# Seven block products for a quarter of the K tiles of a feed forward's gate and up

## The chip, the core and the metric

The program runs on one core of a Trainium2 chip. It is one kernel, launched once. Time is device microseconds of that core; a kernel is timed in several runs and the median is given. Here the kernel before takes 2408.33 us (three runs, 2407.59 to 2408.73).

Engines: TensorE (PE) multiplies matrices, VectorE (DVE) and ScalarE (ACT) work on elements, GpSimd (POOL) helps them, and SyncE (SP) issues DMA transfers. Each engine takes its instructions in the order in which they were written for it and waits on semaphores for the others.

## The reference

256 tokens of width 2048 pass through two layers of a first block (a hybrid of banded attention, gated linear attention and memory attention, with a layer norm) and one layer of a second block. The change is in the last step of the second block, and two more places in it come up later: the first projection of the second block and the step from `w_o` to the feed forward.

```python
D_MODEL, SEQ = 2048, 256
D_FF = -(-(8 * D_MODEL) // (3 * 256)) * 256          # 5632
# second block, after its two mixers gave y_a and y_b
h = rms_norm(x, norm_mix_pre);  proj = h @ w_in
...
merged = jax.nn.sigmoid(g_a) * y_a + jax.nn.sigmoid(g_b) * y_b
x = x + rms_norm(merged @ w_o, norm_mix_post)
h = rms_norm(x, norm_ffn_pre)
gate, up = jnp.split(h @ w_ffn_in, 2, axis=-1)
x = x + rms_norm((jax.nn.silu(gate) * up) @ w_ffn_down, norm_ffn_post)
```

Everything is fp32.

## The kernel before

**Numbers.** An fp32 product is made of three matmuls on rounded operands. A matrix tile is split into a high half (a rounding cast on ACT, L272 for weights) and a low half (the rest, a subtraction on DVE, L273); then x_high·w_high, x_high·w_low and x_low·w_high are added up in PSUM (L330 to L332). Activations are split the same way (L354, L355) behind transposes on PE (L377), four of 128x128 into one PSUM bank.

**Tiling.** A product is a list of jobs, one for each 512 columns of a weight matrix, with the 2048 rows as 16 K tiles of 128. The weights stream from HBM: a part is two K tiles by 512 columns, 512 KB, in one slot of 128x1024. For each K tile there are three matmuls for tokens 0 to 127 (t = 0) and three for tokens 128 to 255 (t = 1), so a part is 12 matmuls of 512 columns. The gate and up of the feed forward are eleven units of 512 columns, each a gate job and an up job of 8 parts; the first unit is called the head. Down products follow each group of units.

**Order.** `Builder.run` writes out all instructions in one go. It walks over units (a part, and which t). Before a unit's matmuls it makes sure that the part is loaded and split; after that `ahead` loads and splits parts in advance, as long as the rules allow: at most N_RAW = 4 loaded and not yet split, at most N_HL = 6 held as split halves, and enough free slots of the 41. Side work (transposes, norms, silu) runs in generators that `pump` steps after each unit, when their time on a planner's clock has come. So the place of an instruction in its engine's order is fixed by when `run`, `ahead` and `pump` reach it.

**Apart.** Where a product begins right behind another whose normalised output it reads, the first tokens are ready sooner than the others. There a run of parts is done apart: first all parts for t = 0 alone, 6 matmuls each, then the same parts for t = 1 (key "in" from `w_out` of the second layer to `w_in` of the second block, "ffn" from `w_o` to the feed forward's head, and the last down columns). The split halves have to be kept for the second pass. In these units `ahead` has its own rule:

```python
if len(units[u][2]) == 1:
    cap, reserve, far = len(parts), 0, u + NEAR
```

The cap on held halves is lifted, no slots are kept in reserve, and splits reach at most NEAR = 8 units ahead. The finishing work between the two products runs on DVE, ACT and POOL: L1467 (squares with a row sum), L1477, L446, L447 (the reciprocal root), L1481 (scaling), L1501 (gain) and, behind that, four transposes; then L542, four squares of the residual for each half of the tokens. In "in" it is a layer norm: L1108, L1109, the transposes, and later L1113 (DVE), L1117 (ACT), L1121 (POOL).

Of the kernel before, what the change touches and what calls it, by code (L numbers as in the profile page):

```python
# [45 lines left out]
FS = 8000  # L46
FH = 4000
# [10 lines left out]
class Job:  # L58
# [11 lines left out]
    def __init__(self, kind, w, c0, cn, act, post, pre=None, order=None, k0=0, apart=None):  # L70
# [3 lines left out]
        self.apart = apart or (None, 0, 0)  # L74
# [23 lines left out]
class Builder:  # L98
    def __init__(self, ctx, tc, a):
        self.tc, self.nc, self.a = tc, tc.nc, a  # L100
        pool = lambda name, bufs, **kw: ctx.enter_context(tc.tile_pool(name=name, bufs=bufs, **kw))
        self.const = pool("const", 1)
        self.tmp = pool("tmp", 2)
        self.small = pool("small", 4)
        self.psm = pool("psm", 2, space=bass.MemoryType.PSUM)
        self.pss = pool("pss", 4, space=bass.MemoryType.PSUM)
        self.dram = pool("dram", 1, space=bass.MemoryType.DRAM)
        self.free = list(range(N_SLOT))
        self.act = self.const.tile([P, NKT, 2, S], F32R, tag="act", name="act")
# [3 lines left out]
        self.clock = 0.0  # L113
        self.n = 0
# [6 lines left out]
    def alloc(self, n=1, dt=F32):  # L121
        tries = 0
        while len(self.free) < n:
            tries += 1
            assert self.side and tries < 1000, "out of slots"
# [87 lines left out]
    def run(self, jobs, loaded_first, split_first):  # L213
# [4 lines left out]
        for job in jobs:  # L218
            n = NKT if job.kind == "n" else min(1024 // job.cn, 4)
            name, lo, hi = job.apart  # L220
            for j, k in enumerate(range(0, len(job.order), n)):
                key = name if lo <= j < hi else None
                if not (key and groups and groups[-1][0] == key):
                    groups.append((key, []))
                groups[-1][1].append(len(parts))
                parts.append((job, job.order[k:k + n], k))
        for key, mine in groups:
            for ts in ((0,), (1,)) if key else ((0, 1),):
                for i in mine:
                    job, kts, k = parts[i]  # L230
                    units.append((job, i, ts, k == 0 and ts[0] == 0, k + len(kts) == len(job.order), mine[-1]))
# [6 lines left out]

        def pieces(i, n):

            return [slice(k, k + 1) for k in range(n)] if i == 0 else [slice(0, n)]

        def do_load(i):
            job, kts, _ = parts[i]
# [8 lines left out]

        def do_split(i):
            job, kts, _ = parts[i]
            n = len(kts) * job.cn
# [19 lines left out]
        def room(u):  # L276
# [4 lines left out]
            if loaded <= end:  # L281
                return len(self.free) > 2
            coming = 2 * max(0, end + 1 - split) - sum(r <= end for r in raws)
            return len(self.free) - coming > HOLD

        def ahead(u):
# [17 lines left out]
        for u, (job, i, ts, first, last, _) in enumerate(units):  # L304
            while split <= i:
                if loaded == split:
# [4 lines left out]
            if len(ts) == 2:  # L311
                ahead(u)
            if first:
                if job.pre:
                    job.pre()
            if first:
                job.ps = self.psm.tile([P, 2, 512], F32, tag="main", name=f"main_j{jobs.index(job)}")
# [3 lines left out]
            for k, kt in enumerate(kts):  # L321
# [4 lines left out]
                if job.kind == "x":  # L326
                    for t in ts:
                        o = job.ps[:, t, :job.cn]
                        rows = slice(t * P, t * P + P)
                        nc.tensor.matmul(o, xh[:, rows], h[:, k, :], start=st, stop=False)  # L330
                        nc.tensor.matmul(o, xh[:, rows], l[:, k, :], start=False, stop=False)  # L331
                        nc.tensor.matmul(o, xl[:, rows], h[:, k, :], start=False, stop=en)  # L332
# [15 lines left out]
            self.pump()  # L348

# [31 lines left out]
def network(ctx, tc, a):  # L381
# [76 lines left out]
    def feeder(act, t, delay, gap=1500):  # L458
        yield delay
        while act.left[t]:  # L460
            act.feed_next(t)
            yield gap

# [1028 lines left out]
    def mix_done(ids, t):  # L1492
# [13 lines left out]
        else:  # L1506
            start_late(fact, [f[0], f[1]], x1res, None, lambda: B.release(ids + f["wi"]), False)
# [36 lines left out]
    def hidden(c, gi):  # L1544

        yield FH
# [32 lines left out]
    for g, n in enumerate((4, 4, 3)):  # L1579
        for c in range(n):  # L1580
            c0 = 512 * (at + c)
            head = (g, c) == (0, 0)
            jobs.append(Job("x", wf, c0, 512, fact, first_gate if head else post_gate2, apart=("ffn", 0, 8) if head else None))
# [63 lines left out]
```

## Time and profile before

| | |
|---|---|
| median of three runs | 2408.33 us (2407.59 to 2408.73) |
| the profiled run, its own time | 2407.96 us |
| span in the profile | 2406.2 us |
| PE busy | 2390.2 us, 99 %, 12105 matmuls and transposes |
| DVE busy | 1476.3 us, 61 % |
| ACT busy | 1099.0 us, 46 % |
| POOL busy | 400.8 us, 17 % |
| from HBM | 454.18 MB read, 192 GB/s over the span |
| DMA engines, share of time on SP's queue | 60.7 % |

All times are of one profiled execution. An engine is busy while it executes an instruction; issuing DMAs and waiting on semaphores isn't counted. Matmuls overlap in the array and their ends are modelled, so the distance between two starts tells what one costs. An idle time is put down to the instruction whose semaphore came last. The granted clock is TensorE's, as a share of full speed.

### The profile page before, as it was taken

What the parts mean: (1) busy time and instruction counts of PE and PEld (TensorE: products, weight loads), DVE (VectorE), ACT (ScalarE), POOL (GpSimd) and SP (SyncE); (2) the same over time, 40 slices, a digit from 0 to 9 for tenths busy, and PEclk for the clock granted to TensorE, in tenths of its full rate; (3) what the DMA queues carried; (4) which work ended last, traced back from release to release, by engine and by line L of the source; (5) the groups of instructions that cost most, each with busy time, mean ns of one, the idle gap of its engine ahead of it and who ended that gap; (6) DMA issues with size and microseconds to landing.
All of it is one profiled execution on the core that took longest, in us unless ns stands there. A gap on an engine that the chain in (4) does not pass through costs nothing. (4 is left out here: it accounts for less than half of the span.)

```text
span 2406.2 us, 31460 instructions
## 1 busy us (share of the span) xinstructions
PE 2390.2 (99%) x12105; PEld 2015.7 (84%) x12105; DVE 1476.3 (61%) x1671; ACT 1099.0 (46%) x1472; POOL 400.8 (17%) x601
## 2 busy tenths in 40 slices
PE   9999999999999999999999999999999999999998
PEld 8888888888888888888888888888888888888886
DVE  6587567666855667766765656657545544554455
ACT  6444445345454553655544544445434423443433
POOL 0330010004400110364764340001000000000000
PEclk9999999999999999999999999999999999999999
DMA  9646567674656674854654666675755655555653
GB/s 327 184 149 184 173 187 262 209 239 133 188 160 186 206 252 156 275 164 125 185 161 146 201 185 194 202 242 186 242 176 180 194 185 193 201 183 177 209 192 131
DMA packets 313911, 464.64 MB, mean 193 GB/s; under 512 B 21961, under 2 KB 161569, under 8 KB 313761
## 3 DMA queue, kind: packets, MB, share of 16 engines
q1 hardware_dynamic: 312528, 459.48, 60.7%
q8 instruction: 95, 1.56, 0.3%
q0 software_dynamic: 640, 2.10, 0.2%
q10 hardware_dynamic: 592, 1.06, 0.1%
q14 instruction: 56, 0.45, 0.1%
HBM read 454.18 MB, written 8.40 MB: 192 GB/s over the span
## 5 line engine op out<-in xcount | busy, mean ns | idle before, releaser
L273 DVE TENSOR_TENSOR slot<-slot,slot 128x1024 fp32r<-128x1024 f32 x810 | 1006.9, 1287 | 190.5 <-ACT slot L272 186.7
L272 ACT CAST slot<-slot 128x1024 fp32r<-128x1024 f32 x810 | 807.8, 1046 | 266.2 <-DVE slot L273 123.6
L339 PE MATMUL main_j<-act,slot 128*128 128x512 f32 x1824 | 651.0, 400 | 0.0
L330 PE MATMUL main_j<-slot,act 128*128 128x512 f32 x1608 | 636.2, 396 | 0.0
L331 PE MATMUL main_j<-slot,act 128*128 128x512 f32 x1608 | 626.4, 390 | 2.8 <-DVE slot L273 2.8
L332 PE MATMUL main_j<-slot,act 128*128 128x512 f32 x1608 | 626.8, 390 | 0.0
L340 PE MATMUL main_j<-act,slot 128*128 128x256 f32 x1824 | 509.9, 280 | 0.0
L339 PEld LDWEIGHTS main_j<-act,slot 128*128 128x128 f32 x1824 | 342.4, 188 | 80.2 <-issue 1.1
L331 PEld LDWEIGHTS main_j<-slot,act 128*128 128x128 f32 x1608 | 302.4, 188 | 63.6 <-DVE slot L273 3.8
L332 PEld LDWEIGHTS main_j<-slot,act 128*128 128x128 f32 x1608 | 301.8, 188 | 63.9
L330 PEld LDWEIGHTS main_j<-slot,act 128*128 128x128 f32 x1608 | 302.2, 188 | 61.3 <-ACT slot L272 0.5
L340 PEld LDWEIGHTS main_j<-act,slot 128*128 128x128 f32 x1824 | 344.1, 189 | 0.8
L330 PE MATMUL main_j<-slot,slot 128*128 128x512 f32 x600 | 236.1, 394 | 0.0
L332 PE MATMUL main_j<-slot,slot 128*128 128x512 f32 x600 | 233.8, 390 | 0.0
L331 PE MATMUL main_j<-slot,slot 128*128 128x512 f32 x600 | 233.6, 389 | 0.0
L447 POOL TENSOR_TENSOR rsl<-rsl,nhalf 128x1 f32<-128x1 f32 x8 | 6.2, 775 | 991.7 <-DVE rsl L446 991.7
L332 PEld LDWEIGHTS main_j<-slot,slot 128*128 128x128 f32 x600 | 112.6, 188 | 23.8
L330 PEld LDWEIGHTS main_j<-slot,slot 128*128 128x128 f32 x600 | 112.7, 188 | 23.0
L331 PEld LDWEIGHTS main_j<-slot,slot 128*128 128x128 f32 x600 | 112.8, 188 | 22.5
L674 POOL TENSOR_TENSOR slot<-slot 128x128 f32<-128x128 f32 x144 | 79.2, 581 | 191.9 <-PE main_j L339 92.8
L354 ACT CAST slot<-bank 128x512 fp32r<-128x512 f32 (+1 forms) x30 | 15.9, 529 | 177.7 <-PE bank L377 170.7
L813 POOL TENSOR_TENSOR slot<-slot,tz 128x512 f32<-128x512 f32 x20 | 25.8, 1290 | 397.8 <-DVE tz L812 397.8
(193 smaller groups left out, 1738.4 us busy)
## 6 DMA issues: line engine op xcount, KB each, us to landing
slot<-in_w_in_dram SPq DMA_DIRECT2D x384, 512.0 KB, 4.0
slot<-in_w_ffn_in_dram SPq DMA_DIRECT2D x176, 512.0 KB, 4.6
slot<-in_w_ffn_down_dram SPq DMA_DIRECT2D x88, 512.0 KB, 4.6
slot<-in_w_out_dram SPq DMA_DIRECT2D x64, 512.0 KB, 4.7
slot<-in_w_o_dram SPq DMA_DIRECT2D x32, 512.0 KB, 4.5
slot<-in_w_mem_kv_dram SPq DMA_DIRECT2D x31, 512.0 KB, 5.9
slot<-in_w_up_b_dram SPq DMA_DIRECT2D x16, 512.0 KB, 4.6
slot<-in_w_up_a_dram SPq DMA_DIRECT2D x16, 512.0 KB, 4.4
```

The source lines that it names most:

```text
L272: nc.scalar.copy(h, src)
L273: nc.vector.tensor_tensor(l, src, h.bitcast(F32), ALU.subtract)
L330: nc.tensor.matmul(o, xh[:, rows], h[:, k, :], start=st, stop=False)
L331: nc.tensor.matmul(o, xh[:, rows], l[:, k, :], start=False, stop=False)
L332: nc.tensor.matmul(o, xl[:, rows], h[:, k, :], start=False, stop=en)
L339: nc.tensor.matmul(job.ps[:, f, :], h[:, k, fs], xs, start=st, stop=False)
L340: nc.tensor.matmul(job.ps[:, f, :S], l[:, k, fs], xh, start=False, stop=en)
L354: nc.scalar.copy(h, src)
L447: G.tensor_tensor(out, out, nhalf[:, :n], ALU.pow)
L674: G.tensor_tensor(view(E[:, l, :]), view(bt), ref, ALU.subtract)
L813: G.tensor_tensor(y, y, tz, ALU.mult)
```

## The change

Ten of the eleven units (all but the head) become a job of a new kind, `Shared`. For K tiles 0 to 11 gate and up go as before. The last four K tiles, 12 to 15, are one block product: the two halves of the tokens by the two pairs of K tiles (12, 13 and 14, 15), times the two pairs of K tiles by gate and up. Two by two blocks need eight products of the usual kind; Strassen's scheme, in Winograd's form, takes seven, here called d, c, a, T1, T2, T4 and T3, of 6 matmuls each. It needs sums of weight blocks, sums of activation blocks, and sums of the products:

- The weight blocks are loaded as before (b and a of the first pair of K tiles, d and c of the second; a and c belong to gate, b and d to up), split, and then added to each other in SBUF by four DMA transfers that accumulate, on POOL's queue: a += b, b += d, d += a, c += d. The four results are split too, so a unit has 19 splits and not 16.
- The activation sums are made once (`combos_of`: five instructions on POOL, one on DVE, one split).
- The products a, T1, T2 and T3 get four PSUM banks of their own; d, c and T4 go straight onto the gate's or up's sums. Three copies on ACT for up and the first product, two for gate, and eight operations on DVE put them together in SBUF.
- The silu, which was part of the jobs' end, moves into the generator `hidden` for these units: it waits FG2 on the planner's clock, then computes, then waits twice FH before the transposes. While the banks are held, `alloc` steps no generator, and after each unit `pump` rests for 4000 of the planner's clock.

In `ahead` the two lines on units with one t are gone; the cap gets one more for each a part held, and loads are counted against what the next splits want. The remaining differences are names and line numbers (L272 is now L356, L354 is L504, L330 to L332 are L439 to L441, L542 is L712).

```diff
+class Shared:
...
+        seq = own(self.b, slice(0, 1)) + mine("d") + own(self.b, slice(1, 2)) + mine("a") + own(self.b, rest)
+        seq += own(self.a, slice(0, 1)) + mine("c") + own(self.a, slice(1, None))
...
     def pump(self):
+        if self.clock < self.quiet:
+            return
...
+        def add(out, x):
+            nc.gpsimd.dma_start(self.s(out), self.s(x), accum_op=ALU.add)
...
+        def sums(job, name, q):
+            at = lambda x: raws[index[id(job), x, q]]
+            if name == "a":
+                a, d = at("a"), at("d")
+                b = raws[("b", index[id(job), "a", q])]
+                add(a, b)
+                add(b, d)
+                add(d, a)
+            elif name == "c":
+                add(at("c"), at("d"))
...
+                key = {"T1": at("a"), "T2": at("d"), "T3": ("b", at("a")), "T4": at("c")}.get(name, i)
+                hls[i] = self.alloc(2, F32R)
+                self.split_to(*(self.s(x) for x in hls[i]), self.s(raws[key]))
+                sums(job, name, q)
...
         def ahead(u):
             cap, nraw, reserve, far = N_HL, N_RAW, RESERVE, len(units)
-            if len(units[u][2]) == 1:
-                cap, reserve, far = len(parts), 0, u + NEAR
+            cap += sum(parts[j][0].kind == "s" and parts[j][1][0] == "a" for j in hls)
             if u < 8:
                 cap, nraw = min(cap, 2 + u), min(nraw, 1 + u)
             while True:
-                if loaded < len(parts) and len(raws) < nraw and room(u):
+                wanted = need[split - 1] if split else 0
+                if loaded < len(loads) and loaded - wanted < nraw and room(u):
                     do_load(loaded)
                     loaded += 1
-                elif split < loaded and len(hls) < cap and len(self.free) > reserve + 1 and first_use[split] <= far:
+                elif split < len(parts) and need[split] <= loaded and len(hls) < cap and len(self.free) > reserve + 1 and first_use[split] <= far:
                     do_split(split)
                     split += 1
...
+    def shared(self, job, name, q, hl):
...
+        for k in range(2):
...
+            self.three(o, xh, xl, hl[0][:, k, :], hl[1][:, k, :], fresh and k == 0, last and k == 1 and name not in "cd")
...
+        if name == "a":
+            A.copy(m1, o)
+        elif name == "T2":
+            V.tensor_tensor(u, o, m1, ALU.add)
+            V.tensor_tensor(w, job.m["T1"], u, ALU.add)
+            V.tensor_tensor(gb[:, 0], gb[:, 0], w, ALU.subtract)
+        elif name == "T4":
+            for t in range(2):
+                A.copy(ga[:, t], ps_a[:, t])
+        elif name == "T3":
+            V.tensor_tensor(v, o, u, ALU.add)
+            V.tensor_tensor(u, o, w, ALU.add)
+            V.tensor_tensor(ga[:, 0], ga[:, 0], m1, ALU.add)
+            V.tensor_tensor(ga[:, 1], ga[:, 1], v, ALU.add)
+            V.tensor_tensor(gb[:, 1], gb[:, 1], u, ALU.subtract)
+            self.held, self.quiet = False, self.clock + 4000
...
-    def hidden(c, gi):
-        yield FH
+    def hidden(c, gi, ui=None):
+        yield FH if ui is None else FG2
+        if ui is not None:
+            for t in range(2):
+                sg, g, r = B.ttile([P, 512], "tz"), vt(gi)[:, t, :], rs2[:, t:t + 1]
+                A.activation(sg, g, AF.Sigmoid, scale=r)
+                V.scalar_tensor_tensor(g, g, r, sg, ALU.mult, ALU.mult)
+                V.scalar_tensor_tensor(g, vt(ui)[:, t, :], r, g, ALU.mult, ALU.mult)
+            B.release([ui])
+            yield 2 * FH
```

How the order moves, first on ACT at the head of the feed forward, in the pass for t = 0. In the kernel before, five casts of weights (L272) stand ahead of the four evictions of the other tokens' transposes (L354, from a bank into `act`), and the squares (L542) come last:

```order
989 L272 CAST slot_14523<-slot_14443 128x1024
990 L272 CAST slot_14536<-slot_14462 128x1024
991 L272 CAST slot_14548<-slot_14481 128x1024
992 L272 CAST slot_14560<-slot_14500 128x1024
993 L272 CAST slot_14572<-slot_14527 128x1024
994 L354 CAST act<-bank_14582 128x4x128
995 L354 CAST act<-bank_14595 128x4x128
996 L354 CAST act<-bank_14608 128x4x128
997 L354 CAST act<-bank_14621 128x4x128
998 L542 ACTIVATE tz_14642,ss_2465_14637<-slot_13822 128x512
999 L542 ACTIVATE tz_14644,ss_2465_14637<-slot_13823 128x512
```

In the changed kernel the same place on ACT reads so, with L356 for the casts of weights, L504 for the evictions and L712 for the squares:

```order
987 L356 CAST slot_14511<-slot_14431 128x1024
988 L504 CAST act<-bank_14548 128x4x128
989 L504 CAST act<-bank_14561 128x4x128
990 L356 CAST slot_14568<-slot_14450 128x1024
991 L504 CAST act<-bank_14580 128x4x128
992 L356 CAST slot_14587<-slot_14469 128x1024
993 L504 CAST act<-bank_14599 128x4x128
994 L356 CAST slot_14606<-slot_14488 128x1024
995 L712 ACTIVATE tz_14624,ss_2565_14619<-slot_13822 128x512
996 L712 ACTIVATE tz_14626,ss_2565_14619<-slot_13823 128x512
997 L712 ACTIVATE tz_14628,ss_2565_14619<-slot_13824 128x512
998 L712 ACTIVATE tz_14630,ss_2565_14619<-slot_13825 128x512
```

One cast now stands between two evictions where five stood ahead of all of them. The head of the second block's input projection has the same pattern.

The second place is POOL's order through the feed forward. Before, from the finishing of `w_o` on (L1501, L447) it holds only small reciprocal roots to the end of the program:

```order
479 L1501 TENSOR_TENSOR slot_14350<-slot_13823,slot_13996 128x512
480 L1501 TENSOR_TENSOR slot_14352<-slot_13825,slot_13997 128x512
481 L447 TENSOR_TENSOR rs_140<-rs_140,nhalf 128x2
482 L447 TENSOR_TENSOR rsl_19575<-rsl_19575,nhalf 128x1
483 L447 TENSOR_TENSOR rsl_19657<-rsl_19657,nhalf 128x1
```

After, the activation sums (L620 to L625) and then the accumulating transfers of the first unit (L304, out<-in, slot by slot) follow the same root, now L597:

```order
481 L597 TENSOR_TENSOR rs_140<-rs_140,nhalf 128x2
482 L620 TENSOR_TENSOR slot_14766<-act 128x512 x2
483 L622 TENSOR_TENSOR slot_14767<-slot_14766 128x256
484 L623 TENSOR_TENSOR slot_14767<-slot_14766 128x256
485 L625 TENSOR_TENSOR slot_14767<-slot_14766,slot_14767 128x256
486 L304 DMA slot_14800<-slot_14788 128x1024
487 L304 DMA slot_14788<-slot_14745 128x1024
488 L304 DMA slot_14745<-slot_14800 128x1024
489 L304 DMA slot_14877<-slot_14745 128x1024
```

Each of the last three touches a slot that one before it reads or writes, so the four are one chain; four such rows stand there for each of the ten units.

## Rows read from the trace of the kernel before

**Rows 1.** The page's first part: busy us, share of the span, instructions.

```profile
span 2406.2 us, 31460 instructions
PE 2390.2 (99%) x12105; PEld 2015.7 (84%) x12105; DVE 1476.3 (61%) x1671; ACT 1099.0 (46%) x1472; POOL 400.8 (17%) x601
```

**Rows 2.** Waits of PE: line, releaser: us in total, times, longest.

```profile
PE main_j L331 <- DVE slot L273: 2.8, 3, 1.3
...
PE bank L377 <- DVE slot L1501: 0.4, 1, 0.4
```

**Rows 3.** Timeline of PE, feed forward: start, length, first and last of 54.

```profile
1899.66 0.39 PE L330 MATMUL main_j<-slot,slot 128*128 128x512 f32 x1
...
1911.67 0.39 PE L332 MATMUL main_j<-slot,slot 128*128 128x512 f32 x1
```

**Rows 4.** Lines by form, 1720 to 2340: busy, mean ns; idle before, releasers.

```profile
L273 DVE TENSOR_TENSOR slot<-slot,slot 128x1024 fp32r<-128x1024 f32 x225 | 259.7, 1218 | 7.2 <-ACT slot L272 7.2
...
L272 ACT CAST slot<-slot 128x1024 fp32r<-128x1024 f32 x224 | 222.5, 1051 | 110.5 <-DVE slot L273 60.9 <-DMA slot<-in_w_ffn_in_dram 15.1 <-DMA slot<-in_w_ffn_down_dram 14.7
```

**Rows 5.** Busy us by window; last: PE's granted clock, DMA share, GB/s.

```profile
1800.00:2050.00 250.00, 250.00 (x1119) 206.99 (x1118) 125.86 (x119) 98.82 (x107) 0.00 (x0) 1.00 0.57 181
2050.00:2300.00 250.00, 250.00 (x1119) 206.97 (x1119) 125.08 (x118) 99.08 (x106) 0.00 (x0) 1.00 0.59 192
...
2400.00:2402.00 2.00, 0.00 (x0) 0.00 (x0) 2.00 (x4) 0.00 (x0) 0.00 (x0) 0.50 0.47 174
```

**Rows 6.** DMA issues (KB, median us to landing) and POOL's issuing line L1096.

```profile
slot<-in_w_ffn_in_dram SPq DMA_DIRECT2D x176, 512.0 KB, 4.6
...
xres<-slot POOLq DMA_DIRECT2D x8, 256.0 KB, 3.1
...
L1096 POOL DMA_DIRECT2D xres<-slot x8 | 4.6, 572 | 12.7 <-DVE slot L1094 12.7
```

**Rows 7.** Timeline of PE at the feed forward's head: start, length, idle before.

```profile
1672.90 0.63 PE L377 MATMUL bank<-ident,slot 128*128 128x128 f32 x4 [0.41 <-DVE slot L1501]
1673.29 0.47 PE L330 MATMUL main_j<-slot,act 128*128 128x512 f32 x1
```

**Rows 8.** Timeline of ACT, in `w_o` and at the feed forward's head.

```profile
1600.58 2.94 ACT L272 CAST slot<-slot 128x1024 fp32r<-128x1024 f32 x3
...
1657.46 0.59 ACT L354 CAST act<-bank 128x512 fp32r<-128x512 f32 x1 [0.99 <-PE bank L377]
1657.94 1.05 ACT L272 CAST slot<-slot 128x1024 fp32r<-128x1024 f32 x1
...
1673.57 0.59 ACT L354 CAST act<-bank 128x512 fp32r<-128x512 f32 x1 [0.34 <-PE bank L377]
...
1679.53 0.63 ACT L542 ACTIVATE tz<-slot 128x512 f32<-128x512 f32 x1
...
1684.44 1.99 ACT L272 CAST slot<-slot 128x1024 fp32r<-128x1024 f32 x2
```

**Rows 9.** Timeline of DVE, in `w_o` and at the feed forward's head.

```profile
1601.65 2.36 DVE L273 TENSOR_TENSOR slot<-slot,slot 128x1024 fp32r<-128x1024 f32 x2 [0.24 <-ACT slot L272]
...
1668.37 3.78 DVE L1481 SCALAR_TENSOR_TENSOR slot<-slot,rsl,slot 128x512 f32<-128x512 f32 x4 [0.67 <-POOL rsl L447]
...
1674.37 5.75 DVE L273 TENSOR_TENSOR slot<-slot,slot 128x1024 fp32r<-128x1024 f32 x5
```

**Rows 10.** Timeline of PE at the head of the second block's input projection.

```profile
941.32 0.60 PE L377 MATMUL bank<-ident,slot 128*128 128x128 f32 x4
...
943.13 0.60 PE L377 MATMUL bank<-ident,slot 128*128 128x128 f32 x4
...
970.86 0.50 PE L331 MATMUL main_j<-slot,act 128*128 128x512 f32 x1 [1.29 <-DVE slot L273]
```

**Rows 11.** Timeline of DVE and ACT at the same head.

```profile
944.18 5.76 DVE L273 TENSOR_TENSOR slot<-slot,slot 128x1024 fp32r<-128x1024 f32 x5
...
958.51 2.73 ACT L1117 ACTIVATE slot<-slot,rsl 128x512 f32<-128x512 f32 x4 [9.59 <-DVE slot L1113]
```

More of the change, by code (lines that the diff above doesn't have):

```diff
@@ L58, with __init__ @@
 class Job:
[L70 removed]
+    def __init__(self, kind, w, c0, cn, act, post, pre=None, order=None, k0=0, apart=None, open=()):
         self.kind, self.w, self.c0, self.cn = kind, w, c0, cn
@@ L112, in __init__ @@
         self.tokens = {"att": N_ATT, "lin": N_LIN}
-        self.clock = 0.0
+        self.clock, self.quiet, self.held = 0.0, 0.0, False
         self.n = 0
@@ L124, in alloc @@
             tries += 1
-            assert self.side and tries < 1000, "out of slots"
+            assert self.side and tries < 1000 and not self.held, "out of slots"
             self.step_all()
@@ L280, in room @@
                 return len(self.free) > RESERVE
-            if loaded <= end:
+            if loaded < need[end]:
                 return len(self.free) > 2
-            coming = 2 * max(0, end + 1 - split) - sum(r <= end for r in raws)
+            coming = 2 * max(0, end + 1 - split) - sum(type(r) is int and r <= end for r in raws)
             return len(self.free) - coming > HOLD
@@ L305, in run @@
             while split <= i:
-                if loaded == split:
+                while loaded < need[split]:
                     do_load(loaded)
@@ L312, in run @@
                 ahead(u)
+            if job.kind == "s":
+                self.shared(job, *parts[i][1], [self.s(x).rearrange("p (k c) -> p k c", c=512) for x in hls[i]])
+                self.release(hls.pop(i))
+                self.pump()
+                continue
             if first:
@@ L327, in run @@
                     for t in ts:
-                        o = job.ps[:, t, :job.cn]
                         rows = slice(t * P, t * P + P)
-                        nc.tensor.matmul(o, xh[:, rows], h[:, k, :], start=st, stop=False)
-                        nc.tensor.matmul(o, xh[:, rows], l[:, k, :], start=False, stop=False)
-                        nc.tensor.matmul(o, xl[:, rows], h[:, k, :], start=False, stop=en)
+                        self.three(job.ps[:, t, :job.cn], xh[:, rows], xl[:, rows], h[:, k, :], l[:, k, :],
+                                   st, en and t not in job.open)
                 elif job.kind == "n":
@@ L348, in run, with three @@
             self.pump()
+    def three(self, o, xh, xl, h, l, start, stop):
+        nc = self.nc
+        nc.tensor.matmul(o, xh, h, start=start, stop=False)
+        nc.tensor.matmul(o, xh, l, start=False, stop=False)
+        nc.tensor.matmul(o, xl, h, start=False, stop=stop)
+    def shared(self, job, name, q, hl):
+        nc, last = self.nc, q == len(job.quads) - 1
+        ps_a, ps_b = job.a.ps if name != "d" else job.b.ps, job.b.ps
+        if (name, q) == ("d", 0):
+            for quad in job.quads:
+                for kt in quad:
+                    job.act.ensure(kt, (0, 1))
+                    job.act.get(kt)
+            job.combos(0)
+        if (name, q) == ("a", 0):
+            self.held = True
+            job.m = dict(zip(("a", "T1", "T2", "T3"), (self.bank() for _ in range(4))))
+            job.out = self.alloc(2)
+            job.tmp = self.alloc(2)
+            gb = self.s(job.out[1]).rearrange("p (t c) -> p t c", t=2)
+            for t in range(2):
+                nc.scalar.copy(gb[:, t], ps_b[:, t])
+        ka, kb = job.quads[q][:2], job.quads[q][2:]
+        x = {"c": (kb, 0), "a": (ka, 0), "T4": (kb, 1)}.get(name)
+        o = {"c": ps_a[:, 0], "T4": ps_a[:, 1], "d": ps_b[:, 0]}.get(name)
+        fresh = o is None and q == 0
+        if o is None:
+            o = job.m[name]
+        for k in range(2):
+            if x:
+                act = job.act.get(x[0][k])
+                xh, xl = (act[:, j, x[1] * P:(x[1] + 1) * P] for j in range(2))
+            else:
+                n = ("T1", "T2", "T3", "d").index(name)
+                xh, xl = (y[:, n, k, :] for y in job.combos(q))
+            self.three(o, xh, xl, hl[0][:, k, :], hl[1][:, k, :], fresh and k == 0, last and k == 1 and name not in "cd")
+        self.clock += 2 * 3 * 512 * 0.427
+        if not last or name in "cd":
+            return
+        V, A = nc.vector, nc.scalar
+        ga, gb, u, w = (self.s(x).rearrange("p (t c) -> p t c", t=2) for x in job.out + job.tmp)
+        m1, u, w, v = u[:, 0], u[:, 1], w[:, 0], w[:, 1]
+        if name == "a":
[14 more added lines that the diff above has]
+            self.held, self.quiet = False, self.clock + 4000
+            self.release(job.tmp)
+            job.post(*job.out)
@@ L1542, in post_up2, with make_fcombos, fcombos, post_both @@
         return post
-    def hidden(c, gi):
-        yield FH
+    QUADS = [(12, 13, 14, 15)]
+    def make_fcombos():
+        for quad in QUADS:
+            f.setdefault("combos", []).append(combos_of(lambda k: B.act[:, k:k + 2], quad))
+            yield 3000
+    def fcombos(q):
+        if f["make"] in B.side:
+            B.drain([f["make"]])
+        return parted(f["combos"][q])
+    def post_both(c):
+        def post(gi, ui):
+            f[("gen", c)] = hidden(c, gi, ui)
+            B.start(f[("gen", c)])
+            f["units"] = f.get("units", 1) + 1
+            if f["units"] * 512 == D_FF:
+                B.release(sum(f["combos"], []))
+        return post
+    def hidden(c, gi, ui=None):
+        yield FH if ui is None else FG2
+        if ui is not None:
+            for t in range(2):
+                sg, g, r = B.ttile([P, 512], "tz"), vt(gi)[:, t, :], rs2[:, t:t + 1]
[4 more added lines that the diff above has]
+            yield 2 * FH
         if len(f["h"]) <= 2 * c:
```

82 lines of the change are left out of this document (76 added, 6 removed).

## Prediction

> **What bounds the kernel now.** First the page's opening part: PE is busy for 2390.2 us of a span of 2406.2, DVE for 61 %, ACT for 46 % [rows 1]. Then the waits of PE over the span: five lines with 6.6 us in all, the largest 2.8 us for DVE's low halves (L273), the smallest 0.4 us for L1501 [rows 2]. So the time changes by matmuls taken out and by new waits of PE, of which there is almost none now. The price of a matmul comes from PE's timeline: 54 matmuls of 512 columns start within 12.01 us, 0.2266 us apart [rows 3] (their "0.39 us" is a modelled length; the pace is what they cost). Six of them, one part for one half of the tokens, are 1.36 us.
>
> Two edits touch time: the block products, and a new rule in `ahead` for the stretches that are run apart (all parts for tokens 0 to 127, then all again for the others). There the cap on held split parts is lifted before; after, it stays at 6.
>
> **The products.** In ten units seven products of 6 matmuls replace eight: 60 matmuls fewer, 60 x 0.2266 = **13.6 us** if all else stays hidden. A unit is then 186 x 0.2266 = 42.1 us. What it adds:
> - Three more splits per unit. A split takes 1.05 us on ACT and 1.22 us on DVE in the feed forward [rows 4], where DVE is busy for 125.9 and 125.1 of 250 us and ACT for 98.8 and 99.1 [rows 5]. After, DVE has per unit 19 x 1.22 = 23 us of splits and twelve operations of half that width (evictions, silu), at most 1.22 us each: below 38 of 42 us. It stays under the bound, so I count nothing; the cover is six split parts, at least 8 us of PE. Without it every unit would be late by up to the three splits, 3.7 us.
> - Four accumulating DMAs of 512 KB per unit on POOL's queue, one chain (a+=b, b+=d, d+=a, c+=d). The trace of before has no DMA that adds. The chain starts about when the unit does, since a's split stands at the front of the order; its last sum is wanted by T4's product 39 us later, less 2.3 us for its split: hidden below some 8.5 us a DMA. Nearest rows: loads of 512 KB land after 4.6 us, 256 KB from POOL's queue after 3.1 us, with 0.57 us to issue [rows 6], at 57 to 59 % of the DMA engines [rows 5]. Low bound: like a load, 4 x 5.2 = 21 us, hidden, cost 0. High bound: two reads for each write, so twice a load, 4 x 9.8 = 39 us, PE late by 2 to 3 us in each of ten units, 20 to 30 us. I take 0, as the row of the same size is the nearer, and keep 30 us for the range. A gain is excluded: no one waited for these before.
> - The Trainium skill ("DMA: Bandwidth & Descriptors", on the anatomy of one DMA, the software path) fits a DMA from GpSimd as 2.0 us plus its bytes over 436 GB/s, by which an estimate is 3.2 us each and 13 us for the chain, hidden too; no run so far shows it for a DMA that adds.
> - The silu now runs in the generator ahead of the transposes, so at three places in the down products the transposes stand right before the matmuls that read them, and PE waits for an eviction: 0.67 us from the transposes' start to the eviction's, 0.59 us of eviction, less twice 0.39 us of transposes [rows 7, 8], 0.5 us: +1.5 us. If they are drained earlier it is 0, at most three times 1.3.
>
> **The apart stretches.** Before, all casts of the first pass stand in ACT's queue ahead of the evictions of the next transposes. After, with six parts held, each further split is issued right before its own matmuls, between those evictions. ACT works in order, and an eviction waits for transposes that stand behind the previous part's matmuls on PE. So ACT can't run ahead, and each part is a chain:
> - transposes' start to the eviction's start: 1672.90 to 1673.57, 0.67 us [rows 7, 8];
> - the eviction's start to that of the cast behind it: 1657.46 to 1657.94, 0.48 us [rows 8];
> - the cast's start to that of DVE's subtraction: 1600.58 to 1601.65, 1.07 us [rows 8, 9], and the subtraction, 1.22 us [rows 4];
> - the five matmuls that wait for the low half, 1.13 us.
> Together 4.57 us, where a part with its transposes now takes 943.13 - 941.32 = 1.81 us [rows 10]: **2.76 us** of waiting for each such part.
>
> Head of the feed forward. Five held parts bring PE to 1672.5; the transposes start at 1672.90 as now, after 0.41 us for L1501, and the sixth part's first matmul at 1673.29 [rows 7]. Its second asks for the low half 0.23 us later. That subtraction stands behind the finishing chain from L1481 on and starts where the first L273 does now, at 1674.37 [rows 9]: result at 1675.6, 2.1 us late. Three parts then go by the chain: 8.3 us. Behind the third cast ACT has four squares, 0.61 us each (eight from 1679.53 to 1684.44 [rows 8]): cast 0.96, squares 2.46, then 2.29 to the low half make 5.7 us after that cast's start; PE asks after 2.29 + 1.13 + 0.23 = 3.65: 2.05 us. Four more squares two parts later cost 1.7 us the same way, with one cast's lead. Sum 14.15, less some 0.3 for before's partly late splits here: **+13.8 us**.
>
> Head of the second block's input projection. The transposes start at 941.32 [rows 10], so the sixth part's low half is asked for at 941.32 + 0.39 + 0.23 = 941.94. It comes behind the layer norm's chain, which ends where L273 starts now, 944.18 [rows 11], or 1.5 us sooner, as fewer subtractions stand ahead of it: 943.9, 1.9 us late. Three parts by the chain: 8.3 us. The last part's subtraction is issued behind four L1113 of 0.7 us (ACT's four L1117 follow them in 2.73 us [rows 11]): three subtractions at 1.15 us' pace, those, and its own put its low half 8.6 us after the first of these casts, against 6.3 asked: 2.3 us. Sum 12.5; the wait of 1.29 us at 970.86 [rows 10] goes, since fewer splits crowd the queue there: **+11.3 us**. In w_out and w_o, where the same rule holds, casts wait for no eviction and run ahead: 0. In the last down column one split stands behind a square: +0.8 us.
>
> Bounds for these 25 us: 0, if ACT did run ahead; 30, if the eviction's own 0.59 us on ACT counts whole and once more on DVE in eight parts. I take the chain, whose links all have rows.
>
> **Sum** against the profiled run's 2407.96 us (1.76 us lie around its span): -13.6 + 0 + 1.5 + 13.8 + 11.3 + 0.8 = +13.8, 2421.8; the median of before is 0.37 us above that run: **2422 us**, 0.57 % slower.
>
> **Rivals.**
> 1. The forecast: late splits cost more than 60 matmuls save. 0.52; its own range is 2414 to 2430.
> 2. The other side: the splits of the apart stretches are covered. Each of the six chained parts that is not late gives back 2.76 us; with five the change is a draw, and with all six and the waits behind the squares and L1113 (2.05 + 1.7 + 2.3) gone it ends at 2422 - 16.6 - 6.1 = 2399. Its place is ACT's queue in the two heads: it needs casts ahead of evictions there. For it: PE shows 6.6 us of waits in all [rows 2], and both other engines have half their time. Against it: each link is an order on one engine, which spare time doesn't loosen. 0.20.
> 3. The sums are late: above 8.5 us a DMA, T4's cast holds all casts behind it on ACT, and PE waits in each of ten units. At 9.8 to 11 us that is 20 to 50 us: 2440 to 2470. For it: ACT already waits 15.1 us in all for loads of w_ffn_in [rows 4], and the sums share the DMA engines with them [rows 5]. Against it: 4.6 us for the same bytes [rows 6]. 0.17. The Trainium skill ("SBUF — State Buffer", on DVE blocking DMA) names another way to it: GpSimd can't write its descriptors while DVE holds the shared port pair in a two-port mode. No row here shows such a delay; what POOL issues takes 0.57 us [rows 6].
> 4. The clock falls in the heads, where PE would be busy 40 % of the time. The granted clock is 1.00 in the feed forward; after PE's last work it is 0.50 at 2400 to 2402 [rows 5], so 1.2 GHz for 2.4. Some 30 us with 12 us of matmuls would then cost 5 to 10 us more: 2430. 0.11.
>
> **From these the numbers.** This kernel's measurement can tell 0.2 % from no change, 4.8 us: 2403.5 to 2413.1. Slower: 1, 3 and 4 nearly whole, 0.71. Faster: most of 2, 0.18. Same: 2 in part, where stalls match the gain, 0.11. The range goes down to 2400, into rival 2, and up to 2452, the late sums' high bound on top of the forecast, and leaves under 2 in 10 out.
>
> **What would show it.** Right: two clusters of PE's waits for DVE's low halves, at about 942 to 966 and 1673 to 1691, three of 2.8 us in each, with 4.6 us from transposes to transposes; and units of 42.1 us. Wrong: no such clusters (rival 2); ACT waiting for the POOL queue's DMAs in every unit, and PE behind it (rival 3); a granted clock below 1.00 in the heads (rival 4). A DVE above 90 % in the units would show that three splits were not free.

## The result and the profile after

The changed kernel takes 2438.14 us (median of 4 runs, 2436.61 to 2438.66), the kernel before 2407.96 us in the same comparison: ratio 1.0123, 95 % interval 1.0108 to 1.0139. It is slower, as forecast, but by 30 us and not by 14. Its profiled span is 2436.9 us, 30.7 more than before's.

The page's first part, as in [rows 1]:

```profile
span 2436.9 us, 31673 instructions
PE 2398.5 (98%) x12045; PEld 2013.0 (83%) x12045; DVE 1568.4 (64%) x1783; ACT 1160.5 (48%) x1553; POOL 442.9 (18%) x646
```

PE has 60 matmuls less and yet 8.3 us more of busy time. That can't be waiting: some matmuls have become longer. The waits of PE (line, releaser: us in total, times, longest), against 6.6 us in all in [rows 2]:

```profile
PE main L440 <- DVE slot L357: 11.8, 13, 2.5
PE main L439 <- ACT slot L356: 10.1, 7, 1.6
PE bank L527 <- DVE slot L1748: 2.5, 2, 1.4
```

Some 19 us of new waits for weight splits, high halves too. PE's timeline says where: at the two heads and nowhere in the feed forward's units. The head of the second block's projection, to compare with [rows 10] (start, length, engine, line, idle before and its releaser):

```profile
942.14 0.60 PE L527 MATMUL bank<-ident,slot 128*128 128x128 f32 x4
...
944.84 0.50 PE L440 MATMUL main<-slot,act 128*128 128x512 f32 x1 [1.87 <-DVE slot L357]
...
946.72 1.05 PE L527 MATMUL bank<-ident,slot 128*128 128x128 f32 x4
949.39 0.79 PE L439 MATMUL main<-slot,act 128*128 128x512 f32 x1 [1.62 <-ACT slot L356]
950.65 0.79 PE L440 MATMUL main<-slot,act 128*128 128x512 f32 x1 [0.47 <-DVE slot L357]
...
952.95 1.05 PE L527 MATMUL bank<-ident,slot 128*128 128x128 f32 x4
...
959.18 1.06 PE L527 MATMUL bank<-ident,slot 128*128 128x128 f32 x4
...
971.29 0.50 PE L440 MATMUL main<-slot,act 128*128 128x512 f32 x1 [2.54 <-DVE slot L357]
```

The chain is there: from transposes to transposes 6.23 us, twice, and as long again to the next part's first matmul (965.42), where before took 1.81. The waits in a link are 1.62 and 0.47 us, less than the 2.76 I gave; but four transposes are 1.05 us long and not 0.60, and matmuls start 0.43 us apart. Busy us by engine of two stretches of the heads, with PE's granted clock, DMA share and GB/s at the end:

```profile
948.00:965.00 17.00, 10.97 (x26) 7.08 (x27) 7.69 (x8) 7.82 (x10) 0.00 (x0) 0.50 0.40 144
1697.00:1716.00 19.00, 12.45 (x32) 7.73 (x30) 6.46 (x7) 8.72 (x16) 0.00 (x0) 0.59 0.42 134
```

The granted clock is at 0.50 in the first stretch, 1.2 GHz, and at it most of the time in the second; before, it was 1.00 outside the program's end.

The units of the feed forward did what they were to do. PE's timeline from one unit's transposes to the same ones of the next, in the changed kernel:

```profile
1817.08 0.60 PE L527 MATMUL bank<-ident,slot 128*128 128x128 f32 x4
...
1860.21 0.60 PE L527 MATMUL bank<-ident,slot 128*128 128x128 f32 x4
```

And in the kernel before:

```profile
1761.44 0.60 PE L377 MATMUL bank<-ident,slot 128*128 128x128 f32 x4
...
1805.93 0.60 PE L377 MATMUL bank<-ident,slot 128*128 128x128 f32 x4
```

43.13 us for 44.49, 1.36 us less a unit, 13.6 us for ten.

Three landmarks of PE's timeline cut the program: the first transposes of the first head (A), those of the feed forward's head (B), and the start of the last matmul (E), in us.

| kernel | A | A to B | B to E |
|---|---|---|---|
| before | 941.32 | 731.58 | 723.58 |
| changed | 942.14 | 750.55 (+19.0) | 734.42 (+10.8) |
| changed, old rule for apart stretches (e1) | 942.29 | 731.52 (-0.1) | 715.96 (-7.6) |
| before, without the old rule (e2) | 941.84 | 749.01 (+17.4) | 741.06 (+17.5) |

The first head costs 19.0 us, the feed forward's head 734.42 - 715.96 = 18.5, and the block products give 7.6 net: 0.8 (A) + 19.0 + 18.5 - 7.6 = 30.7.

### The profile page after: what moved, and what is told of

Same layout as the page of the kernel before. It is cut to its first block, busy times and chain, and to the rows that moved or that the text cites. A ratio compares the mean times of both kernels' runs of the same rounds, so it can differ in the third digit from the quotient of the medians.

```text
span 2436.9 us, 31673 instructions
## 1 busy us (share of the span) xinstructions
PE 2398.5 (98%) x12045; PEld 2013.0 (83%) x12045; DVE 1568.4 (64%) x1783; ACT 1160.5 (48%) x1553; POOL 442.9 (18%) x646
## 4 chain that ended last, share of the span: by engine, by line
PE 55%; DVE 2%; issue 1%; ACT 1%; POOL 1%; DMA 0%; SPq 0%; DVEq 0%; POOLq 0%; ACTq 0%
PE main L440 14%; PE main L441 14%; PE main L439 14%; PE main L426 6%; PE main L427 3%; PE bank L523 2%; DVE slot L357 1%; PE bank L527 1%; PE bank L439 1%; PE bank L441 1%; PE bank L440 1%; ACT slot L356 0%; DMA x1res<-slot 0%; POOL slot L844 0%; PE main L422 0%
## 5 line engine op out<-in xcount | busy, mean ns | idle before, releaser
L357 DVE TENSOR_TENSOR slot<-slot,slot 128x1024 fp32r<-128x1024 f32 x770 | 965.5, 1289 | 275.6 <-ACT slot L356 266.1
L356 ACT CAST slot<-slot 128x1024 fp32r<-128x1024 f32 x770 | 774.9, 1047 | 284.6 <-PE main L440 87.6
L426 PE MATMUL main<-act,slot 128*128 128x512 f32 x1824 | 650.6, 400 | 0.0
L439 PE MATMUL main<-slot,act 128*128 128x512 f32 x1488 | 594.5, 400 | 10.1 <-ACT slot L356 10.1
L440 PE MATMUL main<-slot,act 128*128 128x512 f32 x1488 | 585.8, 394 | 11.1 <-DVE slot L357 11.0
L441 PE MATMUL main<-slot,act 128*128 128x512 f32 x1488 | 584.8, 393 | 0.0
L427 PE MATMUL main<-act,slot 128*128 128x256 f32 x1824 | 509.5, 279 | 0.0
L426 PEld LDWEIGHTS main<-act,slot 128*128 128x128 f32 x1824 | 342.4, 188 | 80.3 <-issue 1.1
L427 PEld LDWEIGHTS main<-act,slot 128*128 128x128 f32 x1824 | 344.0, 189 | 0.7
L440 PEld LDWEIGHTS main<-slot,act 128*128 128x128 f32 x1488 | 282.2, 190 | 72.6 <-DVE slot L357 16.7
L439 PEld LDWEIGHTS main<-slot,act 128*128 128x128 f32 x1488 | 282.1, 190 | 70.0 <-ACT slot L356 13.2
L441 PEld LDWEIGHTS main<-slot,act 128*128 128x128 f32 x1488 | 282.0, 190 | 59.6
L439 PE MATMUL main<-slot,slot 128*128 128x512 f32 x620 | 243.7, 393 | 0.7 <-ACT slot L504 0.7
L440 PE MATMUL main<-slot,slot 128*128 128x512 f32 x620 | 241.5, 390 | 0.8 <-DVE slot L357 0.8
L441 PE MATMUL main<-slot,slot 128*128 128x512 f32 x620 | 241.9, 390 | 0.0
L441 PEld LDWEIGHTS main<-slot,slot 128*128 128x128 f32 x620 | 116.4, 188 | 25.7 <-DVE slot L505 1.3
L304 POOL DMA_DIRECT2D slot<-slot x40 | 35.0, 876 | 563.3 <-DVE slot L505 187.5
L439 PEld LDWEIGHTS main<-slot,slot 128*128 128x128 f32 x620 | 116.4, 188 | 25.2 <-ACT slot L504 1.4
L440 PEld LDWEIGHTS main<-slot,slot 128*128 128x128 f32 x620 | 116.5, 188 | 24.5 <-DVE slot L357 1.1
L505 DVE TENSOR_TENSOR slot<-slot,slot 128x1024 fp32r<-128x1024 f32 (+1 forms) x91 | 98.8, 1103 | 36.5 <-ACT slot L504 36.5
L504 ACT CAST slot<-slot 128x1024 fp32r<-128x1024 f32 (+1 forms) x91 | 85.1, 956 | 50.0 <-DMA slot<-slot 20.7
```

Of the source, the lines that this page charges most:

```text
L304: nc.gpsimd.dma_start(self.s(out), self.s(x), accum_op=ALU.add)
L356: nc.scalar.copy(h, src)
L357: nc.vector.tensor_tensor(l, src, h.bitcast(F32), ALU.subtract)
L426: nc.tensor.matmul(job.ps[:, f, :], h[:, k, fs], xs, start=st, stop=False)
L427: nc.tensor.matmul(job.ps[:, f, :S], l[:, k, fs], xh, start=False, stop=en)
L439: nc.tensor.matmul(o, xh, h, start=start, stop=False)
```

## The experiments

**The old rule put back (e1).**

```diff
+            if len(units[u][2]) == 1:
+                cap, reserve, far = len(parts), 0, u + NEAR
```

> The changed kernel with the old rule for stretches run apart put back into `ahead` (cap lifted, reserve 0, eight units ahead); the block products and everything else stay. Theory A (all of the loss is the late splits in the two heads, with PE at half clock there): the 37 us that the two heads cost in the trace of the changed kernel go, 13.6 us of the products stay less some 5 us given back at the down products: about 2400, 8 us faster than before. Rival B (the block products themselves cost: late sums, DVE, evictions): no better than before, 2408 or above.

2401.12 us (8 runs), ratio to before 0.9972 (0.9962 to 0.9983). Both heads run as before (A to B in the table; the granted clock is 1.00 from 940 to 965 and from 1672 to 1697). Run a second time beside another version:

> The version with the old rule for stretches run apart, once more on the same chip, for the comparison: 2401 again, 7 us below the kernel before.

2400.64 us, ratio 0.9971 (0.9960 to 0.9983). So the block products alone are worth 7 us, and the missing rule cost 37.

**Only the rule taken out of the kernel before (e2).**

```diff
-            if len(units[u][2]) == 1:
-                cap, reserve, far = len(parts), 0, u + NEAR
```

> The kernel before, with only the three lines on units with one t taken out of `ahead`; no block products. Theory A: slower than before by what the two heads cost, 36 to 39 us, about 2445, granted clock 0.50 in parts of both heads, and the wait pattern of the changed kernel there. By my prediction's own terms (late splits at full clock) it would be +25 us, 2433. Rival B: less than +15 us, since the block products make up the rest.

2443.72 us (one run), 35.5 above before: just under theory A's 36 to 39, and far from the 25 of full clock. (The edit takes out two lines, not three.) Its first head, link by link (PE's timeline), has the same pattern with no block product in the program:

```profile
949.01 0.80 PE L328 MATMUL main_j<-slot,act 128*128 128x512 f32 x1 [1.62 <-ACT slot L272]
...
955.25 0.79 PE L328 MATMUL main_j<-slot,act 128*128 128x512 f32 x1 [1.62 <-ACT slot L272]
```

6.24 us a link, at a granted clock of 0.50 (946.33 to 952.57). With e1 this settles the place: the two edits add up, 35.5 - 7.1 = 28.4 of 30.

**PE filled where it waits (e3).** The clock was the open part: is a link 6.2 us because matmuls are slow, or for another reason?

```diff
+                if 5 <= self.nth <= 8:
+                    spare, fill = self.bank(), self.s(hls[self.base][0])[:, :512]
+                    for _ in range(8):
+                        nc.tensor.matmul(spare, job.act.get(0)[:, 0, :P], fill, start=True, stop=True)
```

> The changed kernel with eight matmuls of 512 columns, whose result nobody reads, on PE ahead of four parts in each head (the sixth to ninth of the first pass), where PE waits: 64 matmuls more in all. If the halved clock is what made a chained part 6.2 us and not 4.6: the granted clock stays at 1.00 in the heads, a part takes 4.6 us, and the kernel is some 10 us FASTER for having 64 matmuls more, about 2428. If the clock plays no part and the chain of ACT and DVE alone sets the pace: no change, 2438. If the added matmuls lie on the path: up to 64 x 0.2266 = 14.5 us slower.

2435.08 us (one run), 3 us less with 64 matmuls more. PE's timeline in the first head:

```profile
947.99 2.10 PE L416 MATMUL bank<-slot,act 128*128 128x512 f32 x8
...
951.11 0.50 PE L449 MATMUL main<-slot,act 128*128 128x512 f32 x1 [0.77 <-DVE slot L358]
...
955.86 0.50 PE L449 MATMUL main<-slot,act 128*128 128x512 f32 x1 [0.76 <-DVE slot L358]
...
960.65 0.50 PE L449 MATMUL main<-slot,act 128*128 128x512 f32 x1 [0.77 <-DVE slot L358]
...
968.79 0.79 PE L449 MATMUL main<-slot,act 128*128 128x512 f32 x1 [3.77 <-DVE slot L358]
```

Each bunch of eight lies in the wait, and a link's low half is asked for every 4.8 us. Windows of both heads, as above, with one more behind the links of the first:

```profile
948.00:965.00 17.00, 14.71 (x66) 10.77 (x63) 10.15 (x12) 9.30 (x13) 0.57 (x1) 1.00 0.65 224
968.00:972.00 4.00, 3.21 (x8) 2.53 (x9) 4.00 (x3) 0.72 (x1) 4.00 (x3) 0.50 0.00 0
1696.00:1716.00 20.00, 15.20 (x64) 10.37 (x62) 9.45 (x11) 13.58 (x27) 0.00 (x0) 1.00 0.48 154
```

Through the links the clock stays at 1.00, and a link takes 4.75 and 4.79 us: my 4.57 within about 0.2. That answers the question for the links. The time is a miss: 10 us less were expected. By the landmarks the two heads gave 3.0 and 2.1 us; 1.5 us was lost ahead of A, where the two programs are alike (from 11.6 to 15.0 us the clock was 0.51 in this run and 1.00 in the changed kernel's). In the first head the next wait took part of it: the last part's low half, behind four L1283 on DVE (L1292 in this run), is 3.77 us late (at 968.79) instead of 2.54, and in that wait the clock fell all the same, to 0.50 from 968 to 972. In the second head it stayed at 1.00 to the end.

**No sums (e4).**

```diff
-            nc.gpsimd.dma_start(self.s(out), self.s(x), accum_op=ALU.add)
+            pass
```

> The changed kernel without the 40 accumulating DMAs; the T products read the weight blocks without the sums, so the result is not the feed forward's. Theory A: the sums are hidden, no change, 2438 within 2 us. Rival B (the sums are late, or their traffic delays the loads): faster by 10 us or more.

2434.49 us (one run), 3.7 below the changed kernel, more than the 2 us allowed. The units show that it isn't the sums: from 1812.42 (the mark at 1817.08 above) to the last unit's transposes at 2364.02 are 551.60 us, in the changed kernel 1817.08 to 2368.72, 551.64. The difference lies in the heads, where the clock fell later in this run. That makes its second head a test of the link at full clock with no matmul added (PE's timeline, then the link's window, then the window of the same link in the changed kernel):

```profile
1694.47 0.60 PE L527 MATMUL bank<-ident,slot 128*128 128x128 f32 x4
...
1699.22 0.60 PE L527 MATMUL bank<-ident,slot 128*128 128x128 f32 x4
```

```profile
1694.47:1699.22 4.75, 2.37 (x12) 1.54 (x11) 1.92 (x2) 1.53 (x2) 0.00 (x0) 1.00 0.96 302
```

```profile
1696.99:1703.22 6.23, 4.14 (x11) 2.65 (x10) 1.92 (x2) 1.53 (x2) 0.00 (x0) 0.50 0.92 295
```

ACT and DVE are busy for the same time in both, and the link takes 4.75 us at a granted clock of 1.00 and 6.23 at 0.50. The sums are hidden in full.

**Six sums for four (e8).**

```diff
                 add(b, d)
+                add(b, d)
                 add(d, a)
+                add(d, a)
```

> The version with the old rule for stretches run apart, with b += d and d += a each done twice, six accumulating DMAs a unit for four (so the sums, and the result, are others). One takes 6.8 us to land there and 0.9 us to issue, so a chain of six is some 45 us and the last sum is wanted some 37 us after the chain's start: if the cover ends where I put it, at 8.5 us x 4 = 34 us of chain, PE is late by about 8 us in each of ten units, 40 to 80 us slower than 2401. If the sums have more room than that: within 2 us of 2401.

2475.33 us (one run), 74 above e1. In e1 the four DMAs of one unit stand so on POOL:

```profile
1756.83 0.87 POOL L304 DMA_DIRECT2D slot<-slot  x1 [24.40 <-DMA slot<-in_w_ffn_in_dram]
1762.54 0.87 POOL L304 DMA_DIRECT2D slot<-slot  x1 [4.83 <-DMA slot<-slot]
1772.25 0.87 POOL L304 DMA_DIRECT2D slot<-slot  x1 [8.84 <-DMA slot<-slot]
1777.40 0.87 POOL L304 DMA_DIRECT2D slot<-slot  x1 [4.28 <-PE main L442]
```

With 6.8 us to landing (median) that is 27 us of chain. ACT's waits for these DMAs in e1 (us in total, times, longest):

```profile
ACT slot L506 <- DMA slot<-slot: 19.0, 9, 6.0
```

In e8:

```profile
ACT slot L508 <- DMA slot<-slot: 152.4, 18, 13.1
```

And PE's, for the split behind them, in e8:

```profile
PE main L443 <- ACT slot L508: 38.5, 9, 7.4
```

19 us of ACT's waiting cost PE 0.5 us; with two links more the cover is gone. The bound of the forecast, about 8.5 us for each of four, stood in the right region. The two transfers more are also more traffic, which was not tried apart.

**Two more split parts held (e7).**

```diff
+            cap += 2 * (len(units[u][2]) == 1)
```

> The changed kernel with two more split parts held in units of one t (cap 8 and not 6), nothing else of the old rule. If each part split between two evictions costs its own 4.4 us (6.24 less 1.82): two of three such parts go in each head, 4 x 4.4 = 17.7 us, 2420; at full clock it would be 4 x 2.76 = 11 us, 2427. If it is the reserve of slots or the reach of eight units that holds the splits back: no change, 2438.

2414.14 us (one run), 24 below the changed kernel: more than the 17.7 expected. A to B is 738.67, so the first head costs 7.1 us and not 19. Its transposes stand 1.8 us apart again, and what is left is the end of the pass:

```profile
950.08 0.50 PE L440 MATMUL main<-slot,act 128*128 128x512 f32 x1 [1.67 <-ACT slot L356]
951.34 0.50 PE L441 MATMUL main<-slot,act 128*128 128x512 f32 x1 [0.76 <-DVE slot L357]
...
959.48 0.50 PE L441 MATMUL main<-slot,act 128*128 128x512 f32 x1 [3.72 <-DVE slot L357]
```

So for these 24 us it is the number of held parts, not the reserve of slots or the reach; what the other 13 us to e1 hang on was not tried apart. Two parts more take away the first wait as well as two links, which I had not counted.

**The silu sooner everywhere (e5).** On e1, to win back what the products lose on the way.

```diff
-FG2 = 6000
+FG2 = 1000
...
-            yield 2 * FH
+            yield FH
...
-            self.held, self.quiet = False, self.clock + 4000
+            self.held, self.quiet = False, self.clock + 1000
```

> The version with the old rule for stretches run apart, and the silu of a unit sooner: FG2 1000 for 6000, one FH for two before the transposes, and pump resting for 1000 and not 4000 after a unit. If the 6 us that the products' 13.6 us lose on the way are PE's waits at the three places where transposes stand right before the matmuls that read them (0.9, 0.9 and 3.5 us in that version's trace), these go: 2397. If the silu then takes DVE from the splits that PE needs at a unit's end: no gain, or slower, 2401 to 2405.

2409.84 us (11 runs), ratio 1.0007 (0.9998 to 1.0016): all of the gain is lost, more than either case expected. PE now waits for the silu's last operation at the transposes of seven of the ten units, twice each, since they are issued closer behind it:

```profile
PE bank L529 <- DVE slot L1750: 11.2, 14, 1.1
```

**The silu sooner for the last unit of a group only (e9).**

```diff
             B.start(f[("gen", c)])
+            for _ in range(2 * last):
+                B.step(f[("gen", c)])
...
-                jobs.append(Shared(gate, up, QUADS, fact, fcombos, post_both(c)))
+                jobs.append(Shared(gate, up, QUADS, fact, fcombos, post_both(c, c == n - 1)))
```

> The version with the old rule for stretches run apart, and the silu of the last unit ahead of each group of down products issued right behind the unit's own evictions, ahead of the next five splits; its transposes and all other units as they were. If the 3.5 us at the last of the three places come from the silu standing behind five subtractions on DVE (5.8 us), that wait goes and the two smaller ones stay: 2398, about 3 us less than the version it is made from. If the five splits, now 3 us later, are what PE then waits for: no gain.

2395.78 us (5 runs), ratio 0.9953 (0.9940 to 0.9965), 4.9 below e1 in the same comparison; 3 were expected. In e1 PE's timeline at the third place is

```profile
2331.65 0.33 PE L529 MATMUL bank<-ident,slot 128*128 128x128 f32 x1 [1.39 <-DVE slot L1750]
2333.10 1.75 PE L529 MATMUL bank<-ident,slot 128*128 128x128 f32 x7 [1.12 <-DVE slot L1750]
2334.68 0.80 PE L441 MATMUL main<-slot,slot 128*128 128x512 f32 x1
```

(The clock is 0.70 there from 2334 to 2338; in the changed kernel the waits are the same, 1.40 and 1.12 us, and the clock is 1.00.) In e9 both waits for the silu are gone, which gives 3.4 us; at the two other places the transposes no longer stand right before their matmuls, 0.75 us each, though the two smaller waits were expected to stay. This is the fastest version, 12 us below the kernel before.

**Two block products a unit (e6).** On e1.

```diff
-    QUADS = [(12, 13, 14, 15)]
+    QUADS = [(8, 9, 10, 11), (12, 13, 14, 15)]
...
+            if u > tight:
+                cap, nraw = 5, 3
```

> The version with the old rule for stretches run apart, and block products for K tiles 8 to 15: two groups of four tiles, 60 more matmuls fewer, 22 splits and eight accumulating DMAs a unit; for slots, at most 5 split parts held and 3 loaded from 30 units before the first such unit on. If PE still sets the pace: 13.6 us more, 2388. DVE: 22 x 1.2 + 12 x 0.7 = 35 of 41 us a unit, and the DMAs' two chains want some 29 us each in 41, so if either sets the pace, or five held parts cover too little: no gain over 2401, or slower.

2558.7 us, ratio 1.0626 (1.0611 to 1.0640), 150 us slower than before. PE's largest wait:

```profile
PE main L444 <- ACT slot L509: 86.4, 11, 12.5
```

And ACT's, for the sums:

```profile
ACT slot L509 <- DMA slot<-slot: 221.0, 22, 18.4
```

Eight sums share one queue of POOL and their chains don't fit a unit; this is rival 3, in a kernel that was not forecast. How much of it the five held parts add was not tried.

## Why the prediction was right or wrong

Right in direction and in mechanism, wrong in size: 2438.1 against 2422, inside the range of 2400 to 2452, but more than twice the forecast loss (30.2 for 13.8).

- **The products, -13.6.** Measured -13.6: 43.13 for 44.49 us a unit.
- **Three more splits a unit, 0.** Right. DVE was busy 157 to 163 of 250 us in the units, and PE waits for no split there.
- **The sums, 0, rival 3 not the case.** Right, by e4 and e8. The price was between my two ends: 6.0 us to landing, where a load has 4.6 and twice a load is 9.2.
- **Transposes right before their matmuls, +1.5.** The places were right, the size 5.2: by PE's timeline of the changed kernel 0.75, 0.75 and 3.7 us more than the same transposes cost before. In e1 the third cost 4.6, since the clock fell there; the 3.5 that the expectations of e5 and e9 give for it leaves that out. I priced only the eviction. At the third place the silu itself was late, behind five subtractions on DVE; the last group has three units and not four, so its last transposes come due after 8 K tiles and not 12. e9, which puts the silu ahead of those subtractions, shows it.
- **The chain, 2.76 us a part.** The links are right: with the clock at 1.00 a part took 4.75 us for my 4.57, in e3 and, with no matmul added, in e4. In the changed kernel it took 6.23.
- **The heads, +11.3 and +13.8: the term that was mis-sized.** Measured 19.0 and 18.5. Of the 12.4 us between, the three linked parts make 5.0 us in the first head (3 x (6.23 - 1.81) = 13.3 for 8.3) and 4.6 in the second, where the links took 6.23, 6.23 and 5.9 us. The rest are mostly matmuls at half clock on either side of them; behind the last wait of the first head alone they cost 1.6 us. In the second head the waits behind the squares came out smaller, 1.0 us for 2.05 and none for 1.7, since slower matmuls asked later.
- **The last down column, +0.8.** Right: 1.0 us (part of the 18.5 above, as it lies between B and E; e1's slower third transposes take 0.9 off that again). PE's timeline in the changed kernel:

```profile
2408.39 0.50 PE L440 MATMUL main<-slot,slot 128*128 128x512 f32 x1 [0.76 <-DVE slot L357]
```

- **Rival 4, the clock.** This is where the forecast failed. I priced every link at full clock and put the clock beside the forecast as another case, with a chance of 0.11, where it belonged into the same sum: in each kernel whose heads had the three links and no matmuls added (this one, e2, e4) the granted clock fell to 0.50 in both heads, and in e1, without the chain, it stayed at 1.00 there. Its price, 5 to 10 us, was about right on top of the chain: 3.6 us in the second head (18.2 in the head itself, for 14.6 in e3) and 4.5 in the links of the first (13.3 for 8.8). Added, not weighed, it gives 2427 to 2432, and with the 4 us of the third transposes 2431 to 2436.
- **Rival 2** is out: no cast ran ahead, each of the six linked parts waited 1.62 us for its own.

e3 tests the sum of the heads as well. Its second head, at a granted clock of 1.00 throughout, runs 14.6 us behind the same matmuls of the kernel before, for 14.15 in the forecast: 2.1 us for the first wait, 8.8 for the three links, 2.0 and 1.6 behind the squares, for 2.1, 8.3, 2.05 and 1.7. At full clock the forecast's terms are right one by one. Its first head is not at full clock to the end: 2.1 for the first wait (1.9), 8.8 for the links (8.3), 4.3 for the last part (2.3), 2.3 for matmuls at half clock behind that wait, which I had not, and 1.7 less for the wait of before that goes (1.3), 15.8 in all. The last part's low half came 10.5 us after the first of the casts that I counted from, in e3 as in the changed kernel, for my 8.6: I had an L1283 and its subtraction at their usual length, and beside POOL they took longer (last section). At half clock PE asks later, so there the same delay shows as 2.8 us.

What stays open is why the clock fell at other moments in runs of nearly the same order.

## What to carry to other kernels

A cap on prepared operands is harmless while the preparing engine runs free; where its queue holds an instruction that waits for the consumer, every part above the cap is prepared in series with its use. Price such a stall at both levels of TensorE's clock (here 2.9 and 4.4 us a part), as part of the same case and not as a rival. When a change carries two edits, price them apart and then try them apart: here one was worth 7 us, and the other, two deleted lines, cost 37.

## What the runs showed of the hardware

- In the changed kernel's first head the granted clock fell behind a wait of PE of 1.87 us (matmuls start 0.43 us apart from 945.44 on) and was 0.50 from 948 to 965, with waits of 1.62 and 0.47 us in every 6.2 and PE busy for 65 % of the time. In e3, with PE busy for 14.71 of 17 us, it was 1.00 in the same stretch. But in e4's second head it stayed at 1.00 through a first wait of 1.86 us and a link with waits of 1.62 and 0.76 us, with PE busy for 2.37 of 4.75 us. So the same waits did not always bring it down; what decides is not shown.
- An operation on DVE can be slower while POOL works on SBUF. DVE's timeline at the first head of the changed kernel (three L1283, the first row, end about where POOL begins):

```profile
965.25 2.07 DVE L1283 SCALAR_TENSOR_TENSOR slot<-slot,mvt,slot 128x512 f32<-128x512 f32 x3
...
968.95 2.28 DVE L357 TENSOR_TENSOR slot<-slot,slot 128x1024 fp32r<-128x1024 f32 x1
971.15 6.85 DVE L1283 SCALAR_TENSOR_TENSOR slot<-slot,mvt,slot 128x512 f32<-128x512 f32 x4
```

POOL's timeline:

```profile
966.89 13.53 POOL L1291 TENSOR_TENSOR slot<-slot,slot 128x512 f32<-128x512 f32 x8 [28.38 <-ACT slot L1287]
```

Beside L1291 the subtraction takes 2.28 us for 1.22, and an L1283 1.71 (6.85 for four) for 0.69 (2.07 for three). Not every operation of POOL does that: beside all of them the median of the subtraction is 1.34 us (104 of them). Why was not tried.
- An accumulating DMA of 512 KB inside SBUF landed after 6.0 us (median of 40) beside 16 loads a unit, and its issue kept POOL for 0.87 us, against 0.57 for a plain one of 256 KB.
